# A diffusion step on one core: modulation steps moved between TensorE and VectorE

## The chip, the core and the metric

The kernel runs on one core of a Trainium2 chip. A core has five engines that run side by side, each with its own queue of instructions: TensorE (PE in the profile, with its weight loads as PEld) multiplies matrices into PSUM, VectorE (DVE) and ScalarE (ACT) do elementwise work, GpSimd (POOL) some more of it, and SyncE (SP) starts transfers; all of them can start transfers between HBM and the on-chip memory SBUF. The metric is the time of one execution in microseconds (us) on the device: the median of three runs of the kernel before is 1942.72 us, from 1942.26 to 1943.35.

## The reference

One layer of a hybrid diffusion model, in float32, for 128 context tokens and 256 latent tokens, width 2048:

```python
mod = silu(cond) @ w_ada + b_ada                 # six vectors of 2048 per condition
sh1, sc1, ga1, sh2, sc2, ga2 = split(mod, 6)
h = rmsnorm(x) * (1 + sc1) + sh1
q, k, v, g, lr_f, lr_b, fo = split(h @ w_in)
o = bidirectional gated linear attention (GLA) of q, k, v with decays from lr_f, lr_b   # 4 heads
o = rmsnorm per head(o) * gla_out_norm * silu(g)
f = real part of the 2-D DFT of fo, per group
gates = sigmoid(h @ w_gate + b_gate)
m = (g_a * (o @ w_br_gla) + g_b * (f @ w_br_four)) @ w_out
x = x + ga1 * rmsnorm(m)
h = rmsnorm(x) * (1 + sc2) + sh2
x = x + ga2 * rmsnorm((silu(h @ w_ffn_gate) * (h @ w_ffn_up)) @ w_ffn_down)
```

There are two conditions, one for the context and one for the latent tokens, so `mod` is a product of a 2 x 2048 matrix with a 2048 x 12288 one: little arithmetic on many weights. The output also holds the final GLA states.

## The kernel before

Activations lie with channels on the 128 partitions and all 384 tokens along the row (`T = 384`). The large products are done in three passes on reduced-precision halves: ScalarE casts a weight tile `raw` of 128x1024 to `whi` (line 300), VectorE makes the rest `wlo = raw - whi` (line 287), and TensorE multiplies `whi` with both halves of the activation and `wlo` with the high one (line 326, tile `pmm`). `whi` and `wlo` have four buffers each, so a weight tile can be made up to four units ahead of its use. A *half unit* is one such weight tile with its 24 matmuls; a *unit* of an output column block has two of them where the contraction is 2048 long, and one where it is 1024 long (the branch units).

The order of each engine's instructions is that in which the code emits them, since the kernel schedules PE, ACT, DVE and POOL by hand. The stages are: the first two modulation vectors with the v, q and k projections; the GLA, interleaved with q, k and merge-gate projections; the rest of the merge gates with the Fourier input; the *output gates* (`("o", i)` in `mix_order`, eight units of two half units, `turn` 0 to 15); the *branch units* (`("a", i)`, sixteen units of one half unit, with the last Fourier units `("b", i)` between them); the output projection; the feed-forward part.

The modulation vectors 2, 3 and 4 are made along the way by the generator `ada_rest` (lines 685 to 723). It works on six pieces of 1024 columns, each of 16 *steps*. A step loads 512 KB of `w_ada` into one of two buffers `adaw` (a transfer on POOL's queue) and then does one of two things:

- on PE, if `on_pe[0]` is true: four matmuls into the PSUM tile `pr` (line 697), which stays open until the piece is done;
- else on DVE: two `scalar_tensor_tensor` rows that add the weighted tile to `adacc` (line 707), or for the first step of a piece two `tensor_scalar` rows (line 705).

After 16 steps comes one turn of the generator without work, then one that adds `adacc` into `pr` on PE (line 718) and copies it on ACT (`adev`, line 667), then the next turn begins with two transposes (`ptm`, line 671) and small DVE rows that write `mods` (lines 676 to 681), and goes on with the first step of the next piece.

The generator is advanced by the loops around it. In the GLA, `side` advances `gla()` and then the modulation by one at the end of each half unit. In the output gates another `side` does so at `turn` 0 to 8 and at 9, 11, 13 and 15. In the branch units the table `TAIL` names the units that begin with a step, with True for PE and False for DVE. The output projection runs through what is left.

In the output gates, each odd half unit is followed by `gcol`: transposes of the GLA output (`pt`, line 1196), a Silu on ACT (line 1198), and on DVE `gs` (line 1199) and `o_lo`. A Fourier unit `four(i)` (lines 1239 to 1252) follows from the third output gate on behind each half unit. Its weight tile is folded by VectorE first (`ws`, lines 243 and 244), and then cast and split like the others. In the branch units VectorE multiplies the gate with the product (line 1296), adds (line 1297) and makes `A_lo`, the low half of the output projection's input.

Of the kernel before, what the change touches and what calls it, by code (L numbers as in the profile page):

```python
# [37 lines left out]
XU = 2  # L38
GF = 25
GD = 256  # L40
TAIL = {1: True, 4: False, 5: True, 8: True, 10: False, 11: True, 13: True, 14: False, 15: False}


C_TRI = 0
# [63 lines left out]
def tile_step(ctx: ExitStack, tc: tile.TileContext, a, o):  # L108
# [209 lines left out]
    def step(side):  # L318
        if side is not None:
            next(side, None)  # L320
# [27 lines left out]
    def proj(pool, x, dst, side=None, mid=()):  # L348

        p = pool.tile([P, T], F32, tag="mm", name="pmm")  # L350
        for g in range(2):
            gemm(p, grab(), x, 8, k0=8 * g, first=g == 0, last=g == 1)
            while later:
                later.pop()()
            if g:
                later.append(lambda: dst(p))
            step(side)
            if not g:
                for unit in mid:
                    unit()  # L360
# [5 lines left out]
    def paced(gen, rate):  # L366

        due = 0.0
        while True:
            due += rate[0]  # L370
            while due >= 1.0:
                due -= 1.0
                if next(gen, 1) is not None:
                    return
            yield
# [307 lines left out]
    on_pe = [False]  # L683
# [68 lines left out]
    ada = paced(ada_gen, rate)  # L752
    with ExitStack() as s:
# [22 lines left out]
        def chunks(x):  # L776
            return x.rearrange("p (t c i) -> p t c i", t=3, c=2)

        def gla():
# [10 lines left out]
            for h in range(NH):  # L790
# [38 lines left out]
                for d in range(2):  # L829


                    bT = pss.tile([P, T], F32, tag="side", name="bT")
                    for t in range(3):
                        for j, l in enumerate((lah, lal)):
                            PE.matmul(
                                bT[:, t * P : (t + 1) * P], l[:, t, d], tri[:, d * P : (d + 1) * P],
                                start=j == 0, stop=j == 1,
                            )
                    sx = pss.tile([P, 2, P], F32, tag="side", name="sx")
                    for j, l in enumerate((lah, lal)):  # L840
                        PE.matmul(
                            sx, tri[:, (2 + d) * P : (3 + d) * P], l[:, 0 : 2 + d : 1 + d, d], start=j == 0, stop=j == 1,
                        )
                    eb = pg.tile([P, T], F32, tag=f"eb{d}", name="eb")
                    ACT.activation(eb, bT, AF.Exp)
                    ki = pg.tile([P, T], F32, tag=f"ki{d}", name="ki")
                    ACT.activation(ki, bT, AF.Exp, scale=-1.0)
                    ko = pg.tile([P, 2, P], F32, tag=f"ko{d}", name="ko")
                    ACT.activation(ko, sx, AF.Exp)
                    qi = pg.tile([P, T], F32, tag=f"qi{d}", name="qi")  # L850
                    DVE.scalar_tensor_tensor(qi, eb, DK**-0.5, qT[:, h, :], op0=ALU.mult, op1=ALU.mult)
                    DVE.tensor_mul(ki, ki, kT[:, h, :])
                    DVE.tensor_mul(ko, ko, krs[:, 0 : 2 + d : 1 + d, :])

                    last = 0 if d else CH - 1
                    tot = chunks(eb)[:, :, d, last : last + 1]
                    kc = pg.tile([P, 3, CH], F32, tag=f"kc{d}", name="kc")
                    DVE.tensor_mul(kc, chunks(ki)[:, :, d, :], tot.to_broadcast([P, 3, CH]))
                    dc = pg.tile([P, 1], F32, tag=f"dc{d}", name="dc")
                    c = 5 if d else 2  # L860
                    e0, e1 = c * CH + last, (c + 1 - 2 * d) * CH + last
                    DVE.tensor_mul(dc, eb[:, e0 : e0 + 1], eb[:, e1 : e1 + 1])
                    qin.append(qi)
                    kin.append(ki)
                    kcr.append(kc)
                    kout.append(ko)
                    dec.append((tot, dc))
                    yield

                ats = []  # L870
                for d in range(2):
# [89 lines left out]
        for c in range(2):  # L961
# [4 lines left out]
            DVE.tensor_scalar_mul(dst, up.bitcast(F32), coef[0:98, 1:2])  # L966
            DVE.scalar_tensor_tensor(dst, raw, coef[0:98, 0:1], dst.bitcast(F32), op0=ALU.mult, op1=ALU.add)
        gl = gla()
        def side():
            while True:  # L970
                next(gl, None)
                next(ada, None)
                yield

        sd = side()
# [117 lines left out]
    with ExitStack() as s:  # L1093
# [83 lines left out]
        turn = [0]  # L1177

        def side():
            while True:  # L1180
                on_pe[0] = turn[0] > 6 and turn[0] != 8
                if turn[0] < 9 or turn[0] % 2:
                    next(ada_gen, None)
                on_pe[0] = False
                turn[0] += 1
                next(df, None)
                next(nw, None)
                yield
# [71 lines left out]
        for b, i in mix_order:  # L1260
# [18 lines left out]
            else:  # L1279
# [3 lines left out]
                if i == KT - 3:  # L1283
                    depth[0] = 2
                    spare_raws.clear()
                if i in TAIL:
                    on_pe[0] = TAIL[i]
                    next(ada_gen, None)
# [21 lines left out]
    with ExitStack() as s:  # L1310
# [518 lines left out]
        ada = paced(ada_last(), rate)  # L1829
        pd_tiles, hid_last, x1b, done = None, None, None, 0  # L1830
        for kind, c, i in steps[:-4]:
# [8 lines left out]
            if kind == "D":  # L1840
# [9 lines left out]
                h = hid_last if last_c else hid  # L1850
# [248 lines left out]
```

## Time and profile before

| | |
|---|---|
| median of three runs | 1942.72 us (1942.26 to 1943.35) |
| the profiled execution | 1942.28 us |
| its span, first to last instruction | 1940.4 us |
| granted TensorE clock, mean | 0.998 of full speed |
| steps on PE in the output gates and branch units | 5 and 5 |
| steps on DVE in the output gates and branch units | 6 and 4 |

A page of the profile gives busy times of the engines; its other views list groups of equal instructions, waits and what ended them, the chain of work that ended last, and rows in order of time. A row of the timeline has its start in us, its length, the engine, the line of the code, the operation, the tiles written and read, their shape, how many equal ones were merged, and in brackets the idle time of that engine just before, with what ended it. The end of a row can lie up to 0.1 us behind the start of the next on VectorE and ScalarE, and more on TensorE, since these work on in a pipeline. A busy TensorE is not TensorE at its peak.

### The profile page before, as it was taken

What the parts mean: (1) busy time and instruction counts of PE and PEld (TensorE: products, weight loads), DVE (VectorE), ACT (ScalarE), POOL (GpSimd) and SP (SyncE); (2) the same over time, 40 slices, a digit from 0 to 9 for tenths busy, and PEclk for the clock granted to TensorE, in tenths of its full rate; (3) what the DMA queues carried; (4) which work ended last, traced back from release to release, by engine and by line L of the source; (5) the groups of instructions that cost most, each with busy time, mean ns of one, the idle gap of its engine ahead of it and who ended that gap; (6) DMA issues with size and microseconds to landing.
All of it is one profiled execution on the core that took longest, in us unless ns stands there. A gap on an engine that the chain in (4) does not pass through costs nothing.

```text
span 1940.4 us, 27538 instructions
## 1 busy us (share of the span) xinstructions
PE 1920.4 (99%) x10534; PEld 1690.8 (87%) x10534; DVE 1647.8 (85%) x2172; ACT 916.3 (47%) x1298; POOL 85.8 (4%) x154
## 2 busy tenths in 40 slices
PE   9999999999999999999999999999999999999997
PEld 5779999999999999999988888888888888888886
DVE  5668898889878887978789888999998999888885
ACT  4235455545456554456455444444444444444444
POOL 0001111100000000104000000000000000000001
PEclk9999999999999999999999999999999999999999
DMA  9977766766757885755264636363636272625243
GB/s 390 387 260 248 240 234 227 248 231 194 225 185 246 302 302 181 245 193 198 83 195 131 200 103 194 121 211 98 216 104 213 91 222 93 201 76 185 87 173 110
DMA packets 200615, 380.52 MB, mean 196 GB/s; under 512 B 14196, under 2 KB 126932, under 8 KB 196132
## 3 DMA queue, kind: packets, MB, share of 16 engines
q1 hardware_dynamic: 181252, 320.84, 48.9%
q0 software_dynamic: 13952, 50.39, 8.5%
q10 hardware_dynamic: 5280, 7.55, 1.1%
q8 instruction: 82, 1.34, 0.3%
q14 instruction: 49, 0.40, 0.1%
HBM read 361.94 MB, written 16.78 MB: 195 GB/s over the span
## 4 chain that ended last, share of the span: by engine, by line
PE 93%; DVE 3%; DMA 2%; issue 1%; ACT 1%; SPq 0%; DVEq 0%; ACTq 0%
PE pgu L338 30%; PE pmm L326 30%; PE pdn L338 18%; PE pv L491 3%; PE pgm L474 1%; PE pf L1239 1%; PE pfo L1039 1%; DVE adacc L707 1%; PE pmm L1516 1%; PE ptr L1808 1%; PE pf L1240 1%; PE pfo L1040 1%; DMA xraw<-in_w_x 1%; PE po L788 1%; PE px L509 0%
## 5 line engine op out<-in xcount | busy, mean ns | idle before, releaser
L326 PE MATMUL pmm<-A_hi,whi 128*128 128x384 f32 x1072 | 361.7, 337 | 0.0
L326 PE MATMUL pmm<-A_hi,wlo 128*128 128x384 f32 x1072 | 358.8, 335 | 0.0
L326 PE MATMUL pmm<-A_lo,whi 128*128 128x384 f32 x1072 | 358.6, 335 | 0.0
L1663 ACT CAST whi<-u 128x1024 fp32r<-128x1024 f32 x200 | 210.6, 1053 | 281.5 <-DVE u L1647 86.5
L1663 ACT CAST whi<-raw 128x1024 fp32r<-128x1024 f32 x175 | 184.2, 1052 | 200.8 <-PE pgu L338 63.8
L1674 DVE TENSOR_TENSOR wlo<-u,whi 128x1024 fp32r<-128x1024 f32 x200 | 244.1, 1220 | 32.0 <-ACT whi L1663 18.3
L338 PE MATMUL pgu<-whi,A_hi 128*128 128x512 f32 x640 | 250.0, 391 | 0.0
L338 PE MATMUL pgu<-whi,A_lo 128*128 128x512 f32 x640 | 249.3, 389 | 0.0
L1674 DVE TENSOR_TENSOR wlo<-raw,whi 128x1024 fp32r<-128x1024 f32 x175 | 213.4, 1220 | 34.6 <-ACT whi L1663 25.6
L287 DVE TENSOR_TENSOR wlo<-raw,whi 128x1024 fp32r<-128x1024 f32 x163 | 198.2, 1220 | 24.1 <-ACT whi L300 23.7
L300 ACT CAST whi<-raw 128x1024 fp32r<-128x1024 f32 x149 | 156.0, 1051 | 117.6 <-PE pmm L326 50.0
L326 PEld LDWEIGHTS pmm<-A_hi,whi 128*128 128x128 f32 x1072 | 201.2, 188 | 3.3 <-issue 2.5
L326 PEld LDWEIGHTS pmm<-A_lo,whi 128*128 128x128 f32 x1072 | 201.4, 188 | 0.2
L326 PEld LDWEIGHTS pmm<-A_hi,wlo 128*128 128x128 f32 x1072 | 201.2, 188 | 0.3 <-DVE wlo L287 0.2
L707 DVE SCALAR_TENSOR_TENSOR adacc<-adaw,spad,adacc 128x1024 f32<-128x1024 f32 x160 | 198.1, 1279 | 3.5 <-DMA adaw<-in_w_ada 3.2
L338 PE MATMUL pdn<-whi,hid_hi 128*128 128x512 f32 x480 | 186.9, 389 | 0.0
L338 PE MATMUL pdn<-whi,hid_lo 128*128 128x512 f32 x480 | 186.8, 389 | 0.0
L338 PE MATMUL pgu<-wlo,A_hi 128*128 128x512 f32 x640 | 184.2, 389 | 0.0
L338 PEld LDWEIGHTS pgu<-whi,A_hi 128*128 128x128 f32 x640 | 120.2, 188 | 26.1 <-issue 0.8
L338 PEld LDWEIGHTS pgu<-wlo,A_hi 128*128 128x128 f32 x640 | 120.1, 188 | 25.4
L338 PEld LDWEIGHTS pgu<-whi,A_lo 128*128 128x128 f32 x640 | 120.1, 188 | 25.0
L338 PE MATMUL pgu<-whi,S 128*128 128x512 f32 x480 | 131.1, 395 | 0.0
(405 smaller groups left out, 3042.7 us busy)
## 6 DMA issues: line engine op xcount, KB each, us to landing
adaw<-in_w_ada POOLq DMA_DIRECT2D x96, 512.0 KB, 4.0
raw<-in_w_d SPq DMA_DIRECT2D x88, 512.0 KB, 3.7
slab<-in_w_ada SPq DMA_DIRECT2D x32, 1024.0 KB, 10.2
raw<-in_w_gate SPq DMA_DIRECT2D x64, 512.0 KB, 4.4
raw<-in_w_g SPq DMA_DIRECT2D x48, 512.0 KB, 3.4
raw<-in_w_u SPq DMA_DIRECT2D x48, 512.0 KB, 3.5
raw<-in_w_in SPq DMA_DIRECT2D x44, 512.0 KB, 4.3
u<-in_w_u SPq DMA_DIRECT2D x40, 512.0 KB, 4.6
```

The source lines that it names most:

```text
L287: eng.tensor_sub(lo, raw, hi.bitcast(F32))
L300: ACT.copy(hi, raw)
L326: PE.matmul(dst, w[wi][:, k * n + n0 : k * n + n0 + P], x[xi][:, k0 + k, :], start=first and k == 0 and j == 0, stop=last and k == kts - 1 ...
L338: PE.matmul(dst, stat[x_][m], mov(w[w_], m), start=first and w_ == m == x_ == 0, stop=last and w_ == m == 1,)
L474: PE.matmul(pgv[q : q + 32, :], spad[:, k, :], slab[k // (KT // 2)][:, k % (KT // 2), :], start=k < 4, stop=k >= KT - 4,)
L491: PE.matmul(pv[2 * t + g], hT[x_][:, kb, t * P : (t + 1) * P], w_[:, g * 512 : (g + 1) * 512], start=kb == 0 and j == 0, stop=kb == KT - 1 ...
L707: DVE.scalar_tensor_tensor(acc[:, c, :], w, spad[:, k, c : c + 1], acc[:, c, :], op0=ALU.mult, op1=ALU.add,)
L788: PE.matmul(dst, w[wi], x[xi], start=first and j == 0, stop=last and j == 2)
L1039: PE.matmul(p, w_of[0][:, i, k, g, :], x[:, :, lo:hi], start=kt == 0, stop=False)
L1040: PE.matmul(p[:, 0], w_of[1][:, i, k, g, :], x[:, 0, lo:hi], start=False, stop=kt == KT - 1)
L1663: ACT.copy(hi, src)
L1674: DVE.tensor_sub(lo, src, hi.bitcast(F32))
```

## The change

```diff
-TAIL = {1: True, 4: False, 5: True, 8: True, 10: False, 11: True, 13: True, 14: False, 15: False}
+TAIL = {1: False, 4: False, 5: False, 7: False, 8: False, 10: False, 11: False, 13: False, 14: False, 15: False}
@@ in gla(), the loop over the two directions d of a head h
                     dec.append((tot, dc))
-                    yield
+                    yield h == 0 and d == 0
@@ in side() of the GLA stage
-                next(gl, None)
-                next(ada, None)
+                if not next(gl, None):
+                    next(ada, None)
@@ in side() of the output gates
-                on_pe[0] = turn[0] > 6 and turn[0] != 8
+                on_pe[0] = turn[0] > 12
```

In the GLA stage one half unit of the first head, the one that prepares direction 0, no longer takes a step. All later turns of the generator come one place later, until the new entry 7 in `TAIL` brings it level again; behind unit 7 of the branch units the same step is done at the same place as before. The choice of engine changes as well:

| place | steps before | steps now |
|---|---|---|
| first GLA head, direction 0 | 1 on DVE | none |
| output gates, `turn` 0 to 4 | 5 on DVE | 5 on DVE |
| `turn` 5 | a turn without work | 1 on DVE |
| `turn` 6 | `adacc` into `pr`, copy `adev` | a turn without work |
| `turn` 7 | `mods`, first step of a piece, on PE | `adacc` into `pr`, copy `adev` |
| `turn` 8 | 1 on DVE (line 705) | `mods`, first step of a piece, on DVE (line 705) |
| `turn` 9 and 11 | 2 on PE | 2 on DVE |
| `turn` 13 and 15 | 2 on PE | 2 on PE |
| branch units 1, 5, 8, 11, 13 | 5 on PE | 5 on DVE |
| branch unit 7 | none | 1 on DVE |
| branch units 4, 10, 14, 15 | 4 on DVE | 4 on DVE |

So eight steps go from PE to DVE. Where the rows stand on VectorE is shown at three places. The first is the first GLA head, between the rows of direction 0 (`kc`, `dc`) and those of direction 1 (`qi`):

```order
 L858 TENSOR_TENSOR kc<-ki,eb 128x192
 L862 TENSOR_TENSOR dc<-eb 128x1
-L707 SCALAR_TENSOR_TENSOR adacc<-adaw,spad,adacc 128x1024 x2
 L287 TENSOR_TENSOR wlo<-raw_1706,whi 128x1024
 L851 SCALAR_TENSOR_TENSOR qi<-eb,qk 128x384
```

The step ahead of the weight split and of direction 1 is gone. The second place is VectorE in the output gates around `turn` 9, from the fold of a Fourier weight (`ws`) to the weight splits, before and then now:

```order
L243 TENSOR_TENSOR ws<-raw 128x512
L244 TENSOR_TENSOR ws<-raw 128x512
L1199 SCALAR_TENSOR_TENSOR gs<-gs,gnorm,pt 128x384
L379 TENSOR_TENSOR o_lo<-gs,o_hi 128x384
L287 TENSOR_TENSOR wlo<-ws,whi 128x1024
L287 TENSOR_TENSOR wlo<-raw,whi 128x1024
```

```order
L243 TENSOR_TENSOR ws<-raw 128x512
L244 TENSOR_TENSOR ws<-raw 128x512
L707 SCALAR_TENSOR_TENSOR adacc<-adaw,spad,adacc 128x1024 x2
L1199 SCALAR_TENSOR_TENSOR gs<-gs,gnorm,pt 128x384
L379 TENSOR_TENSOR o_lo<-gs,o_hi 128x384
L287 TENSOR_TENSOR wlo<-ws,whi 128x1024
L287 TENSOR_TENSOR wlo<-raw,whi 128x1024
```

The step stands between the fold and `gs`; it does so at `turn` 5, 9 and 11. The third place is VectorE in the branch units, from the last row of Fourier unit 13 to the weight splits behind branch unit 8, before and then now:

```order
L1252 TENSOR_TENSOR y<-y,gate 128x384
L243 TENSOR_TENSOR ws<-raw 128x512
L244 TENSOR_TENSOR ws<-raw 128x512
L1296 TENSOR_TENSOR gate<-gate,pmm 128x384
L1297 TENSOR_TENSOR yb<-yb,gate 128x384
L379 TENSOR_TENSOR A_lo<-yb,A_hi 128x384
L287 TENSOR_TENSOR wlo<-ws,whi 128x1024
L287 TENSOR_TENSOR wlo<-raw,whi 128x1024
```

```order
L1252 TENSOR_TENSOR y<-y,gate 128x384
L707 SCALAR_TENSOR_TENSOR adacc<-adaw,spad,adacc 128x1024 x2
L243 TENSOR_TENSOR ws<-raw 128x512
L244 TENSOR_TENSOR ws<-raw 128x512
L1296 TENSOR_TENSOR gate<-gate,pmm 128x384
L1297 TENSOR_TENSOR yb<-yb,gate 128x384
L379 TENSOR_TENSOR A_lo<-yb,A_hi 128x384
L707 SCALAR_TENSOR_TENSOR adacc<-adaw,spad,adacc 128x1024 x2
L287 TENSOR_TENSOR wlo<-ws,whi 128x1024
L287 TENSOR_TENSOR wlo<-raw,whi 128x1024
```

The step of unit 7 is new, and that of unit 8 comes from TensorE: between these two Fourier units VectorE now has two steps where it had none.

## The prediction

> **What bounds the kernel.** The page first: shares of busy time, and the chain that ended last.
>
> ```profile
> PE 1920.4 (99%) x10534; PEld 1690.8 (87%) x10534; DVE 1647.8 (85%) x2172; ACT 916.3 (47%) x1298; POOL 85.8 (4%) x154
> PE 93%; DVE 3%; DMA 2%; issue 1%; ACT 1%; SPq 0%; DVEq 0%; ACTq 0%
> ```
>
> TensorE (PE) is the bound nearly everywhere, so work taken off it counts in full, as long as VectorE (DVE) keeps up. The change does take work off PE, and gives it to DVE. So the second view is busy time by stage: the first GLA head, the output gates from half unit 4 on, the branch units, the start of the output projection.
>
> ```profile
> core 0: us, PE busy (x) PEld busy (x) DVE busy (x) ACT busy (x) POOL busy (x), PEclk, DMA share, GB/s
> 145.00:195.00 50.00, 48.45 (x313) 47.69 (x312) 42.99 (x51) 26.14 (x36) 5.02 (x10) 1.00 0.73 249
> 571.00:655.00 84.00, 84.00 (x553) 79.75 (x554) 71.62 (x143) 53.98 (x85) 3.69 (x7) 1.00 0.74 243
> 655.00:738.00 83.00, 83.00 (x514) 79.87 (x513) 73.15 (x123) 41.01 (x68) 4.74 (x9) 1.00 0.88 309
> ```
>
> In both stages that receive steps PE never pauses, but DVE has only 12.4 us (84.00 - 71.62) and 9.9 us (83.00 - 73.15) free. Whether a step fits there is the whole question.
>
> **Prices of one step.** On PE, from the timeline in the branch units:
>
> ```profile
> 708.32 0.33 PE L326 MATMUL pmm<-o_lo,whi 128*128 128x384 f32 x1
> 708.49 0.34 PE L326 MATMUL pmm<-o_hi,wlo 128*128 128x384 f32 x1
> 708.76 0.64 PE L697 MATMUL pr<-adaw,spad 128*32 128x256 f32 x8
> 709.33 0.45 PE L326 MATMUL pmm<-o_hi,whi 128*128 128x384 f32 x1
> ```
>
> From the last matmul before it to the first after it are 0.84 us, against a pitch of 0.17: a step costs PE 0.67 us. On DVE, a step and the row behind it, and then the load that it needs (issue to landing):
>
> ```profile
> 706.88 2.47 DVE L707 SCALAR_TENSOR_TENSOR adacc<-adaw,spad,adacc 128x1024 f32<-128x1024 f32 x2
> 709.27 0.69 DVE L243 TENSOR_TENSOR ws<-raw 128x512 f32<-128x512 f32 x1
> adaw<-in_w_ada POOLq DMA_DIRECT2D x96, 512.0 KB, 4.0
> ```
>
> A step costs DVE 709.27 - 706.88 = 2.39 us. Eight steps move: 8 x 0.67 = 5.4 us come off PE, 8 x 2.39 = 19.1 us go onto DVE, and as one GLA step goes, the two late stages receive nine (three in the output gates, six in the branch units), 21.5 us against 22.3 us of idle time. That looks as if it just fitted; the next parts ask which of that idle time can be used.
>
> **First GLA head: a gain.** VectorE's and TensorE's rows there, then the same products of a later head:
>
> ```profile
> 188.77 2.47 DVE L707 SCALAR_TENSOR_TENSOR adacc<-adaw,spad,adacc 128x1024 f32<-128x1024 f32 x2
> 191.16 1.21 DVE L287 TENSOR_TENSOR wlo<-raw,whi 128x1024 fp32r<-128x1024 f32 x1
> 192.77 0.54 DVE L852 TENSOR_TENSOR ki<-ki,qk 128x384 f32<-128x384 f32 x1
> 191.34 0.57 PE L875 MATMUL at<-qi,ki 128*64 128x64 f32 x12
> 193.46 0.57 PE L875 MATMUL at<-qi,ki 128*64 128x64 f32 x12 [1.55 <-DVE ki L852]
> 193.83 0.71 PE L881 MATMUL cr<-qi,kc 128*64 128x64 f32 x12
> 328.56 0.92 PE L875 MATMUL at<-qi,ki 128*64 128x64 f32 x24
> 329.31 0.52 PE L881 MATMUL cr<-qi,kc 128*64 128x64 f32 x12
> ```
>
> PE waits 1.55 us for `ki`, behind the very step that goes. Without it `ki` ends at 193.31 - 2.39 = 190.92, before the products begin at 191.34. They take 193.83 - 191.34 = 2.49 us here and 0.75 in the later head: **-1.7 us**. The load of that step goes too. All later steps of the GLA move by one half unit; there PE never waits, so I count that as nothing.
>
> **Output gates.** One round is two half units, an even and an odd one, each followed by the Fourier products of one unit; behind the odd one DVE has the row `gs` (L1199), which needs that unit's Silu from ScalarE (ACT). The `gs` at 606.78 is that of half unit 9, the one at 621.01 that of half unit 11. DVE over this round, then ACT's rows at its begin, then the first PE matmul that needs the `wlo` made there:
>
> ```profile
> 606.01 0.69 DVE L244 TENSOR_TENSOR ws<-raw 128x512 f32<-128x512 f32 x1
> 606.78 0.61 DVE L1199 SCALAR_TENSOR_TENSOR gs<-gs,gnorm,pt 128x384 f32<-128x384 f32 x1
> 607.98 0.56 DVE L379 TENSOR_TENSOR o_lo<-gs,o_hi 128x384 fp32r<-128x384 f32 x1 [0.58 <-ACT o_hi L378]
> 608.93 1.23 DVE L287 TENSOR_TENSOR wlo<-ws,whi 128x1024 fp32r<-128x1024 f32 x1 [0.39 <-ACT whi L294]
> 615.59 1.23 DVE L287 TENSOR_TENSOR wlo<-ws,whi 128x1024 fp32r<-128x1024 f32 x1 [1.17 <-ACT whi L294]
> 621.01 0.61 DVE L1199 SCALAR_TENSOR_TENSOR gs<-gs,gnorm,pt 128x384 f32<-128x384 f32 x1
> 606.25 0.49 ACT L1198 ACTIVATE gs<-pmm 128x384 f32<-128x384 f32 x1
> 607.43 0.52 ACT L378 CAST o_hi<-gs 128x384 fp32r<-128x384 f32 x1 [0.68 <-DVE gs L1199]
> 607.85 1.05 ACT L294 CAST whi<-ws 128x1024 fp32r<-128x1024 f32 x1
> 612.53 0.25 PE L1240 MATMUL pf<-edT,wlo 128*128 128x194 f32 x1
> ```
>
> DVE's only pauses in a round (0.58, 0.39, 1.17) are waits for ACT casts that themselves wait for the DVE row just before. DVE and ACT thus form one chain of 621.01 - 606.78 = 14.23 us, as long as PE's round, and a step in front of `gs` lengthens it: the pauses don't shrink. The new steps of half units 9 and 11 stand exactly there: VectorE takes its rows in order, so `gs`, the two casts, both `wlo` and the rows of `y` behind them all move back by the step. Only 0.16 us is free at the first (L244 lets the next row start at about 606.62, `gs` waits until 606.78) and nothing at the second. The cushion is the lead of `wlo`: it ends at 608.93 + 1.23 = 610.16 and is needed at 612.53, so 2.37 us.
>
> Half unit 5 gets a step as well, before a `gs` whose ACT input is ready early; and at half unit 7 the small rows of `mods` leave the place before `gs`:
>
> ```profile
> 577.64 0.61 DVE L1199 SCALAR_TENSOR_TENSOR gs<-gs,gnorm,pt 128x384 f32<-128x384 f32 x1
> 575.76 0.49 ACT L1198 ACTIVATE gs<-pmm 128x384 f32<-128x384 f32 x1 [2.31 <-PE pmm L326]
> 591.80 0.23 DVE L676 COPY mods<-ptm 128x8 f32<-128x8 f32 x2
> 592.33 0.61 DVE L1199 SCALAR_TENSOR_TENSOR gs<-gs,gnorm,pt 128x384 f32<-128x384 f32 x1
> ```
>
> DVE's lateness against the profile: +2.39 (half unit 5); -0.53 where `mods` left (592.33 - 591.80) and +0.45 where it lands in half unit 8; +2.39 - 0.16 (half unit 9); +2.39 (half unit 11): 6.9 us. PE waits for all but the lead: 6.9 - 2.4 = **4.5 us late** when the branch units begin. The 0.67 us that PE saves at half units 7, 9 and 11 only let it come earlier to that wait, so I count them as zero (if that cover is gone, they are worth 2.0 us); so too the `pr` bank that stays free until half unit 13. ACT copies `adev` at half unit 7 instead of 6, ahead of its Silu, which delays the Silu by some 1.1 us; `gs` is later than that anyway.
>
> **Branch units.** DVE's row that waits for PE, all 16 units together, and DVE's last row against the matmul that needs it:
>
> ```profile
> L1296 DVE TENSOR_TENSOR gate<-gate,pmm 128x384 f32<-128x384 f32 x16 | 8.8, 551 | 8.5 <-PE pmm L326 8.5
> 736.47 1.23 DVE L379 TENSOR_TENSOR A_lo<-yb,A_hi 128x384 fp32r<-128x384 f32 x2
> 741.39 0.33 PE L326 MATMUL pmm<-A_lo,whi 128*128 128x384 f32 x1
> ```
>
> Here the idle time is real: 8.5 us of waiting for PE, which vanish once DVE is the later one. Six more steps are 14.3 us, so the lateness grows by 14.3 - 8.5 = 5.8 to 12.7 us. The output projection needs the last `A_lo` at 741.39, and it ends at 737.70: a lead of 3.7. PE is therefore 12.7 - 3.7 = **9.0 us late**, for good, since PE is again the bound from there on. The branch matmuls saved (5 x 0.67) vanish in the wait again. Their loads go out two steps ahead; the shortest notice, two steps before unit 15, is some 7 us against 4.0 to land. SP's weight loads wait for `wlo` to free a buffer and move with DVE, never by more.
>
> **Sum.** +9.0 - 1.7 = +7.3 on the profiled execution, 1942.28 (span 1940.4), which is 0.4 under the median: 1949.6, or about 1949.9 by the median. I say 1949.8. Bounds: the GLA term 0 to -1.9 (the idle 1.55 and what the `cr` row shows over its later twin); the stages from +2.1 (only the branch units cost) to +12.7 (no lead helps).
>
> **Rivals.** *Faster:* DVE swallows the steps, PE keeps 5.4 + 1.7: 1935.6. For it speaks that the sums nearly fit (21.5 in 22.3); against it that 2.1 us of each 14.2 are waits inside DVE's own chain. It decides by whether a lead of 2.37 outlasts a step of 2.39 in front of `gs`. *No change:* the output gates hide their three steps, the branch units alone cost 5.8 - 3.7 = 2.1: 2.1 - 1.7, 1943.1. *Slower still:* the clock falls. New PE pauses near half units 9 and 11 last 1 to 2 us each, at two neighbouring matmuls; if the clock halved after both, the 2.4 us of Fourier products behind each would double: +4.8, 1954.6. Against it: the granted clock is 1.00 in the window that holds the 1.55 us pause. The Trainium skill (TensorE: Matmul & The Clock Gate, Why this matters for your kernels) warns of idle gaps over about 3 us, after which the clock is halved; no run here shows a gap of that length. By that rule my pauses are too short, and the sum stays as it is.
>
> **How the numbers follow.** Likeliest 70%; slower still 9%; no change 11%; faster 10%. A difference under 0.2% (3.9 us) can't be told from none. The range drops the faster case and some of the slowest: 1943 to 1955; the likeliest alone gives 1946.5 to 1953. Slower: 70 + 9 + a little of the no-change case = 0.81; same 0.10; faster 0.09.
>
> **What would show it.** Right: no pause before `at` in the first head; PE pauses at the Fourier products (L1239, L1240) that end with DVE `wlo` or ACT `whi`, 4.5 us in all by the start of the branch units; L1296 no longer waits for PE; DVE almost without idle time from 571 to 750; the output projection starts some 7 us later. Wrong: L1240 still has a positive lead after half unit 9, or L1296 still waits.

## The result, and the profile after

The changed kernel takes 1949.39 us in the median of five runs (1948.73 to 1950.28), against 1942.72. It is slower by 6.7 us; forecast were 7.1. The ratio over all runs is 1.0036, with a 95% interval of 1.0026 to 1.0047 (ratios here and below are over all runs, and differ from those of the medians by up to 0.0003). Its profiled execution took 1950.06 us with a span of 1948.3, so 0.67 more than the median and 7.9 more span than the one before.

First the page of the changed kernel, then busy time in the three stages of the prediction (the third is drawn out to where the changed kernel ends the branch units).

```profile
PE 1920.5 (99%) x10470; PEld 1693.6 (87%) x10470; DVE 1665.3 (85%) x2188; ACT 915.4 (47%) x1298; POOL 85.8 (4%) x154
PE 88%; DVE 6%; DMA 3%; ACT 2%; issue 1%; SPq 0%; DVEq 0%; ACTq 0%
```

```profile
145.00:195.00 50.00, 50.00 (x324) 49.34 (x323) 43.42 (x53) 25.80 (x36) 5.02 (x10) 1.00 0.71 245
571.00:655.00 84.00, 78.57 (x485) 74.79 (x484) 72.55 (x138) 47.61 (x74) 3.43 (x7) 0.96 0.66 215
655.00:745.00 90.00, 86.70 (x508) 86.06 (x507) 88.10 (x140) 44.00 (x75) 5.01 (x10) 0.98 0.91 309
```

PE's busy time over the whole span is the same to 0.1 us although eight steps are gone, since it now also runs at a lower granted clock for a while (0.96 and 0.98 in these windows, 1.00 before); and 5.4 us (84.00 - 78.57) and 3.3 us of idle time have come into two stages that had none. DVE's share of the chain that ended last has doubled to 6%. The view of waits on PE says who is late:

```profile
PE pf L1240 <- DVE wlo L287: 5.6, 5, 1.9
PE pf L1239 <- ACT whi L294: 3.2, 2, 1.7
PE pmm L326 <- DVE wlo L287: 0.4, 1, 0.4
```

(us in total, times, longest.) In the first head the pause before `at` is gone: DVE and PE there, with `ki` written by 190.46 and all 24 matmuls of `at` in one go:

```profile
189.91 0.55 DVE L852 TENSOR_TENSOR ki<-ki,qk 128x384 f32<-128x384 f32 x1
191.05 2.48 DVE L707 SCALAR_TENSOR_TENSOR adacc<-adaw,spad,adacc 128x1024 f32<-128x1024 f32 x2
191.34 0.92 PE L875 MATMUL at<-qi,ki 128*64 128x64 f32 x24
```

In the output gates the rows `gs` are the milestones: those of half units 5, 7, 9, 11, 13 and 15, with three rows of the kernel before behind them.

```profile
578.76 0.61 DVE L1199 SCALAR_TENSOR_TENSOR gs<-gs,gnorm,pt 128x384 f32<-128x384 f32 x1
592.92 0.61 DVE L1199 SCALAR_TENSOR_TENSOR gs<-gs,gnorm,pt 128x384 f32<-128x384 f32 x1
607.56 2.48 DVE L707 SCALAR_TENSOR_TENSOR adacc<-adaw,spad,adacc 128x1024 f32<-128x1024 f32 x2
609.96 0.61 DVE L1199 SCALAR_TENSOR_TENSOR gs<-gs,gnorm,pt 128x384 f32<-128x384 f32 x1
611.14 0.56 DVE L379 TENSOR_TENSOR o_lo<-gs,o_hi 128x384 fp32r<-128x384 f32 x1 [0.58 <-ACT o_hi L378]
612.09 1.23 DVE L287 TENSOR_TENSOR wlo<-ws,whi 128x1024 fp32r<-128x1024 f32 x1 [0.39 <-ACT whi L294]
618.76 1.23 DVE L287 TENSOR_TENSOR wlo<-ws,whi 128x1024 fp32r<-128x1024 f32 x1 [1.17 <-ACT whi L294]
626.56 0.61 DVE L1199 SCALAR_TENSOR_TENSOR gs<-gs,gnorm,pt 128x384 f32<-128x384 f32 x1
641.51 0.62 DVE L1199 SCALAR_TENSOR_TENSOR gs<-gs,gnorm,pt 128x384 f32<-128x384 f32 x1 [0.67 <-ACT gs L1198]
655.74 0.61 DVE L1199 SCALAR_TENSOR_TENSOR gs<-gs,gnorm,pt 128x384 f32<-128x384 f32 x1
```

```profile
554.53 0.61 DVE L1199 SCALAR_TENSOR_TENSOR gs<-gs,gnorm,pt 128x384 f32<-128x384 f32 x1 [2.18 <-PE pt L1196]
635.23 0.62 DVE L1199 SCALAR_TENSOR_TENSOR gs<-gs,gnorm,pt 128x384 f32<-128x384 f32 x1
649.46 0.61 DVE L1199 SCALAR_TENSOR_TENSOR gs<-gs,gnorm,pt 128x384 f32<-128x384 f32 x1
```

The three pauses of a round (0.58, 0.39, 1.17) have not shrunk by a hundredth though a step of 2.48 stands before them. Before the gates begin, `gs` stands 1.27 us earlier than before (553.26 against 554.53). From there it falls back by 2.39 at half unit 5 (578.76 - 577.64 = +1.12), gains 0.53 (592.92 against 592.33), loses 2.59 (609.96 against 606.78), 2.37 (626.56 against 621.01), and 0.73 more (641.51 against 635.23), where no step stands but where `gs` waited 0.67 us for its Silu. In sum 7.55.

PE's pauses there, besides one of 0.64 us at 582.18 behind the step of half unit 5, and the granted clock from one of them on:

```profile
612.11 0.45 PE L1239 MATMUL pf<-edT,whi 128*128 128x388 f32 x1 [1.43 <-ACT whi L294]
613.37 0.36 PE L1240 MATMUL pf<-edT,wlo 128*128 128x194 f32 x1 [0.81 <-DVE wlo L287]
628.71 0.45 PE L1239 MATMUL pf<-edT,whi 128*128 128x388 f32 x1 [1.73 <-ACT whi L294]
629.97 0.53 PE L1240 MATMUL pf<-edT,wlo 128*128 128x194 f32 x1 [0.81 <-DVE wlo L287]
```

```profile
629.97:636.24 6.27, 6.27 (x22) 6.27 (x23) 5.04 (x11) 3.85 (x6) 0.00 (x0) 0.50 0.57 172
...
725.05:728.50 3.45, 3.45 (x15) 3.45 (x15) 3.42 (x5) 1.47 (x3) 0.00 (x0) 0.52 1.01 308
```

Behind the pauses of 1.73 and 0.81 us PE ran 6.27 us at half its clock (22 matmuls, some 3 us more than at full clock), and behind one of 1.85 us in the branch units again for 3.4 us. And the branch units: L1296 over the whole program, and the end of the stage.

```profile
L1296 DVE TENSOR_TENSOR gate<-gate,pmm 128x384 f32<-128x384 f32 x16 | 8.8, 548 | 0.0
733.10 2.48 DVE L707 SCALAR_TENSOR_TENSOR adacc<-adaw,spad,adacc 128x1024 f32<-128x1024 f32 x2
735.50 1.22 DVE L287 TENSOR_TENSOR wlo<-raw,whi 128x1024 fp32r<-128x1024 f32 x1
747.80 1.22 DVE L379 TENSOR_TENSOR A_lo<-yb,A_hi 128x384 fp32r<-128x384 f32 x2
749.25 0.33 PE L326 MATMUL pmm<-A_lo,whi 128*128 128x384 f32 x1
```

L1296 never waits any more. The last `A_lo` is written at 749.02, 11.3 us later than the 737.70 of before, and PE comes to the matmul that needs it at 749.25, 7.86 us later than the 741.39 of before; from there to the end the shift stays as it is (7.9 in the span).

### The profile page after: what moved, and what is told of

It is laid out like the page before. It is cut to its first block, busy times and chain, and to the rows that moved or that the text cites. A ratio compares the mean times of both kernels' runs of the same rounds, so it can differ in the third digit from the quotient of the medians.

```text
span 1948.3 us, 27434 instructions
## 1 busy us (share of the span) xinstructions
PE 1920.5 (99%) x10470; PEld 1693.6 (87%) x10470; DVE 1665.3 (85%) x2188; ACT 915.4 (47%) x1298; POOL 85.8 (4%) x154
## 3 DMA queue, kind: packets, MB, share of 16 engines
q10 hardware_dynamic: 5280, 7.55, 1.1%
## 4 chain that ended last, share of the span: by engine, by line
PE 88%; DVE 6%; DMA 3%; ACT 2%; issue 1%; SPq 0%; DVEq 0%; ACTq 0%
PE pgu L338 30%; PE pmm L326 27%; PE pdn L338 18%; PE pv L491 3%; PE pgm L474 1%; DVE adacc L707 1%; DVE wlo L287 1%; PE pfo L1039 1%; PE pmm L1516 1%; DMA four_d<-y 1%; PE ptr L1808 1%; DMA xraw<-in_w_x 1%; PE po L788 1%; PE pf L1239 0%; PE px L509 0%
## 5 line engine op out<-in xcount | busy, mean ns | idle before, releaser
L326 PE MATMUL pmm<-A_hi,whi 128*128 128x384 f32 x1072 | 362.1, 338 | 0.0
L326 PE MATMUL pmm<-A_hi,wlo 128*128 128x384 f32 x1072 | 359.3, 335 | 0.4 <-DVE wlo L287 0.4
L326 PE MATMUL pmm<-A_lo,whi 128*128 128x384 f32 x1072 | 359.0, 335 | 0.0
L338 PE MATMUL pgu<-whi,A_hi 128*128 128x512 f32 x640 | 250.0, 391 | 0.0
L338 PE MATMUL pgu<-whi,A_lo 128*128 128x512 f32 x640 | 249.3, 389 | 0.0
L707 DVE SCALAR_TENSOR_TENSOR adacc<-adaw,spad,adacc 128x1024 f32<-128x1024 f32 x176 | 217.9, 1280 | 2.8 <-DMA adaw<-in_w_ada 2.5
L326 PEld LDWEIGHTS pmm<-A_hi,whi 128*128 128x128 f32 x1072 | 201.6, 188 | 3.3 <-issue 2.5
L326 PEld LDWEIGHTS pmm<-A_hi,wlo 128*128 128x128 f32 x1072 | 201.5, 188 | 1.0 <-DVE wlo L287 0.9
L326 PEld LDWEIGHTS pmm<-A_lo,whi 128*128 128x128 f32 x1072 | 201.7, 188 | 0.2
L338 PE MATMUL pdn<-whi,hid_hi 128*128 128x512 f32 x480 | 186.9, 389 | 0.0
L338 PE MATMUL pdn<-whi,hid_lo 128*128 128x512 f32 x480 | 186.8, 389 | 0.0
L338 PE MATMUL pgu<-wlo,A_hi 128*128 128x512 f32 x640 | 184.2, 389 | 0.0
L338 PEld LDWEIGHTS pgu<-whi,A_hi 128*128 128x128 f32 x640 | 120.1, 188 | 26.0 <-issue 0.8
L338 PEld LDWEIGHTS pgu<-wlo,A_hi 128*128 128x128 f32 x640 | 120.1, 188 | 25.4
L338 PEld LDWEIGHTS pgu<-whi,A_lo 128*128 128x128 f32 x640 | 120.1, 188 | 25.1
L338 PE MATMUL pgu<-whi,S 128*128 128x512 f32 x480 | 131.1, 395 | 0.0
```

Of the source, the lines that this page charges most:

```text
L326: PE.matmul(dst, w[wi][:, k * n + n0 : k * n + n0 + P], x[xi][:, k0 + k, :], start=first and k == 0 and j == 0, stop=last and k == kts - 1 ...
L338: PE.matmul(dst, stat[x_][m], mov(w[w_], m), start=first and w_ == m == x_ == 0, stop=last and w_ == m == 1,)
L707: DVE.scalar_tensor_tensor(acc[:, c, :], w, spad[:, k, c : c + 1], acc[:, c, :], op0=ALU.mult, op1=ALU.add,)
```

## The experiments

My theory, as in the prediction: VectorE's rows form a chain; a step lengthens it by its 2.39 us unless it stands where VectorE really waits for another engine, and PE pays what the lead doesn't cover. The rivals: VectorE's load alone decides (the steps fit into its idle time or not, wherever they stand); and the halved clock is what costs the time. All medians below are of kernels timed beside the kernel before on the same chip, which took 1942.57 us there (1942.59 in the last group).

**The GLA part alone.** The step that is left over goes to branch unit 7.

```diff
-TAIL = {1: True, 4: False, 5: True, 8: True, 10: False, 11: True, 13: True, 14: False, 15: False}
+TAIL = {1: True, 4: False, 5: True, 7: False, 8: True, 10: False, 11: True, 13: True, 14: False, 15: False}
-                    yield
+                    yield h == 0 and d == 0
-                next(gl, None)
-                next(ada, None)
+                if not next(gl, None):
+                    next(ada, None)
```

> The GLA part alone (the step that it leaves over is added in branch unit 7, on VectorE). My theory: PE no longer waits 1.55 us for `ki` (a gain of 1.7), the changed kernel's new 0.4 us pause before the Fourier-input products comes with it, and the added step of 2.39 us fills idle time of L1296 (4.2 us of it lie in units 6 to 9). In all 1.3 us less: about 1941.4. Rival: the wait only moves to another product, no change, 1942.7. Rival: the added step is not covered, 2.39 - 1.3 = 1.1 more, 1943.8.

Measured: 1941.53 us (1940.58 to 1942.37, 11 runs), ratio 0.9993, interval 0.9984 to 1.0002. It is 1.0 us less, near the 1.3 of my theory, though the interval takes in no change; the trace shows what happened: no wait for `ki`, and one at L326, here of 0.9.

```profile
PE pmm L326 <- DVE wlo L287: 0.9, 1, 0.9
```

That wait, at some 520 us, comes and goes with the execution: it is there with 0.63 us in the next kernel, too, whose GLA is that of before.

**The output gates alone.**

```diff
-                on_pe[0] = turn[0] > 6 and turn[0] != 8
+                on_pe[0] = turn[0] > 12
```

> The output gates alone (branch units and GLA as before). By the step of the prediction, PE is 4.5 us late at the begin of the branch units and nothing there gives it back: 1947.2. If the halved clock that the changed kernel shows after its pause at 626.64 is a real loss, PE is 7.5 us late there (the shift of 6.28 at 635 plus the 1.27 of the GLA), 1950.2. Rival (load: VectorE has 12.4 us free in this stage and swallows three steps of 2.39): PE keeps 3 x 0.67, 1940.7.

Measured: 1948.94 us (1948.76 to 1950.5, 5 runs), ratio 1.0032 (1.0019 to 1.0044): 6.4 more. That VectorE swallows the steps is refuted. The value lies between my two numbers, and the trace shows the same pair of pauses with the clock behind them: first the two matmuls, then the windows on both sides.

```profile
614.13 0.45 PE L1239 MATMUL pf<-edT,whi 128*128 128x388 f32 x1 [1.98 <-ACT whi L294]
615.39 0.36 PE L1240 MATMUL pf<-edT,wlo 128*128 128x194 f32 x1 [0.81 <-DVE wlo L287]
```

```profile
611.00:615.40 4.40, 1.60 (x9) 1.02 (x7) 3.43 (x5) 2.78 (x5) 0.53 (x1) 1.00 0.83 240
615.40:619.60 4.20, 4.20 (x19) 4.20 (x20) 4.13 (x10) 1.87 (x3) 0.00 (x0) 0.61 0.58 181
```

VectorE's `gs` falls back by 6.8 us here (+1.16 at half unit 7, +3.29 at 9, +2.37 at 11): other terms than the prediction's, and nearly its sum. PE begins the branch units 4.6 us late (656.19 against 650.83, in an execution that stood 0.75 us later at the begin of the gates), which is 6.8 less a lead of 2.2, and it is 4.7 late at the matmul with the last `A_lo`. So the theory's 4.5 holds, and the halved clock has cost next to nothing by then: PE was going to wait for VectorE anyway. The rest of the 6.4 comes later: in the profiled execution, the slowest of the five, another 2.8 us come in behind the output projection, of them 1.1 in a wait for `psums` (L338) that only some of the profiles here show.

**Everything but the output gates.**

```diff
-                on_pe[0] = turn[0] > 12
+                on_pe[0] = turn[0] > 6 and turn[0] != 8
```

(against the changed kernel)

> The change without its output-gate part. My theory: six steps of 2.39 less 8.5 idle make VectorE 5.8 us late at the last `A_lo`, less the lead of 3.7 is 2.1, less 1.3 from the GLA: 0.8 more, 1943.5; L1296 no longer waits, and the granted clock stays 1.00 in the output gates. Rival (load): all of it fits, 5 x 0.67 + 1.3 = 4.7 less, 1938.0. Rival: the branch units alone cost the 9.0 us that the prediction gave both stages together, 1950.4.

Measured: 1945.05 us (1944.0 to 1945.81, 11 runs), ratio 1.0010 (1.0001 to 1.0019): 2.5 more, where I had said 0.8. My sum had left out that the GLA part brings a step to half unit 5 of the output gates, in this kernel too. `gs` therefore enters the branch units 2.0 us late (2.39 - 0.53 + 0.19; within the lead, so PE doesn't wait at that place; it does wait 0.64 us at half unit 5), and the sum is 2.0 + 5.0 - 3.7 = 3.3 for PE. The trace has that: PE's matmul with the last `A_lo` but one starts 2.9 us later than before (743.81 against 740.87) in an execution that stood 0.3 us earlier at the begin of the gates, and here it does wait for it.

```profile
743.81 0.44 PE L326 MATMUL pmm<-A_lo,whi 128*128 128x384 f32 x1 [1.09 <-DVE A_lo L379]
```

The 5.0 replaces the prediction's 5.8 (14.3 - 8.5). The idle times shown for L1296 run from the end of the row before, and rows that stand back to back overlap by up to 0.1 us (733.10 + 2.48 = 735.58, while the next begins at 735.50). Each of the nine waits is worth that much more to a later VectorE: 8.5 + 9 x 0.09 = 9.3. In this kernel the clock stayed at 1.00 behind two pauses of 1.85 us, and the loss is still there: here the clock is not what makes it.

```profile
700.00:703.00 3.00, 1.37 (x8) 1.04 (x7) 3.00 (x3) 1.97 (x4) 0.53 (x1) 1.00 0.77 213
703.00:706.50 3.50, 3.28 (x22) 3.28 (x23) 3.47 (x6) 1.11 (x3) 0.00 (x0) 1.00 1.02 336
```

**The branch units alone.** Nine steps as before, all on VectorE.

```diff
-TAIL = {1: True, 4: False, 5: True, 8: True, 10: False, 11: True, 13: True, 14: False, 15: False}
+TAIL = {1: False, 4: False, 5: False, 8: False, 10: False, 11: False, 13: False, 14: False, 15: False}
```

> The branch units alone: the nine steps of before, all on VectorE (five more there), GLA and output gates as before. My theory: 5 x 2.39 = 12.0, less the 9.3 of idle time that the kernel without the output-gate part showed to be usable, makes the last `A_lo` 2.65 us late; PE comes to it 5 x 0.67 = 3.35 earlier; the lead of 3.7 covers 0.35 of the 2.65, so PE waits 2.3 and keeps 1.05: 1941.6. Rival: what the kernel without the output-gate part lost there comes from the six steps themselves (3.3 for six, so some 2.8 for five): 1945.4.

Measured: 1941.47 us (1940.67 to 1942.21, 11 runs), ratio 0.9993 (0.9984 to 1.0002). The forecast was 1941.6, the rival's 1945.4. Five steps more on VectorE in the same stage cost no time; six of them behind a VectorE that enters 2.0 us late cost some 3 us. The difference is the lead: PE waits 1.1 us for the last `A_lo` but one and 1.2 for one `wlo`, and saves five steps of 0.67.

```profile
PE pf L1240 <- DVE wlo L287: 1.2, 1, 1.2
PE pmm L326 <- DVE A_lo L379: 1.1, 1, 1.1
```

**The same steps one half unit later.** The changed kernel, with the VectorE steps of the output gates where a round has its longest pause.

```diff
-                if turn[0] < 9 or turn[0] % 2:
+                if turn[0] < 9 or turn[0] in (10, 12, 13, 15):
```

> The changed kernel, but the VectorE steps of half units 9 and 11 of the output gates stand one half unit later (10 and 12), between a fold `ws` and its `wlo`, where VectorE waits 1.17 us for the cast in each round. My theory (a chain of VectorE and ScalarE rows, not VectorE's load): each of these two steps then lengthens the chain by 2.39 - 1.17 = 1.22 instead of 2.39. VectorE starts the branch units 2.39 - 0.53 + 0.45 + 2 x 1.22 = 4.75 us late (7.55 in the changed kernel), 5.04 more there, less the lead of 3.7: PE 6.1 late, less 1.3 of the GLA: 4.8 more than before, 1947.4, some 3 us under the changed kernel's profiled execution; pauses of PE in the output gates of some 2.4 us in all. Rival (load): the same number of the same rows in the same stage, so the changed kernel's time, 1949.4.

Measured: 1947.24 us (1946.19 to 1947.94, 9 runs), ratio 1.0024 (1.0015 to 1.0034); 1947.4 was forecast by the chain, 1949.4 by load. The row below stands where the wait of 1.17 us was:

```profile
614.03 0.68 DVE L244 TENSOR_TENSOR ws<-raw 128x512 f32<-128x512 f32 x1
614.64 2.47 DVE L707 SCALAR_TENSOR_TENSOR adacc<-adaw,spad,adacc 128x1024 f32<-128x1024 f32 x2
617.03 1.22 DVE L287 TENSOR_TENSOR wlo<-ws,whi 128x1024 fp32r<-128x1024 f32 x1
622.43 0.61 DVE L1199 SCALAR_TENSOR_TENSOR gs<-gs,gnorm,pt 128x384 f32<-128x384 f32 x1
637.77 0.61 DVE L1199 SCALAR_TENSOR_TENSOR gs<-gs,gnorm,pt 128x384 f32<-128x384 f32 x1
```

`wlo` no longer waits, and from one `gs` to the next are 637.77 - 622.43 = 15.34 us instead of 14.23: the step costs the chain 1.11 us, not 2.39. The same work in the same stage, moved by half a round, is worth 2 us; the load is not the price. Nor is it the clock that makes the 1.11: it stays at 1.00 in this profile, and in that of the changed kernel the two steps had cost their 2.59 and 2.37 before it fell.

**Four steps more on VectorE in the branch units,** with the GLA part.

```diff
-TAIL = {1: True, 4: False, 5: True, 8: True, 10: False, 11: True, 13: True, 14: False, 15: False}
+TAIL = {1: False, 4: False, 5: True, 7: False, 8: False, 10: False, 11: True, 13: False, 14: False, 15: False}
```

> GLA as changed, output gates as before, and in the branch units four steps more on VectorE (1, 7, 8, 13), not six; 5 and 11 stay on TensorE. My theory: the idle time of L1296 before and behind these units takes all but 1.5 us of their 9.6, the lead of 3.7 (less the 2.0 that PE saves) covers that, so PE keeps 3 x 0.67 = 2.0 and the 1.3 of the GLA: 3.3 less, 1939.4. Rival: VectorE's idle time is not usable, 9.6 - 3.7 - 1.3 = 4.6 more, 1947.3.

Measured: 1941.13 us (1940.55 to 1942.91, 11 runs), ratio 0.9991 (0.9983 to 1.0000): 1.4 less, not 3.3. The rival that the idle time isn't usable falls; my number was too good: it again left out the 2.0 us of half unit 5, and took 1.3 for the GLA. VectorE enters the branch units 2.0 us late and is 2.2 late at the last `A_lo`, so the four steps cost it 0.25 us there, which is 4 x 2.39 less the 9.3 found above.

**That step of half unit 5 back on PE.** Against the kernel just told:

```diff
-                on_pe[0] = turn[0] > 6 and turn[0] != 8
+                on_pe[0] = turn[0] > 4 and turn[0] not in (6, 8)
```

> The kernel with four steps more on VectorE in the branch units (GLA as changed), and half unit 5's step of the output gates, which the GLA part brought there, on TensorE. My theory: the step costs PE 0.67 and takes away both the pause that it made (0.78 more between two matmuls at 582) and 2.31 us of VectorE's lateness, so that PE no longer waits for the last `A_lo` (0.4 there): 0.5 less than the kernel with four steps more, and no PE pause from 560 on. About 1940.6. Rival: that step was hidden where it was, so this one is 0.67 longer: 1941.8.

Measured: 1940.95 us (1939.47 to 1944.81, 11 runs), ratio 0.9991 (0.9982 to 1.0000). In the trace no PE pause is left between 560 and 745, as forecast, and PE starts the output projection some 3 us earlier than before. Of these, 0.5 remain in the span of that execution: PE waits 0.91 us at 984 and 0.76 at 1886, waits that some of the other profiles here show and some do not. It is the best of all kernels here by its median, 1.6 us under the kernel before; between it and the one with the step on VectorE no difference can be told.

**Which pauses lose the clock.** The kernel before, with pauses put into PE (core of the edit; the last line for the second kernel):

```diff
+        def pause(n):
+            for k in range(2):
+                px_ = pss.tile([P, 64], F32, tag="side", name="pz")
+                PE.matmul(px_, ident, z[:, 0:64], start=True, stop=True)
+                if not k:
+                    for _ in range(n):
+                        POOL.memset(z, 0.0)
...
+                if n > 12 and n % 3 == 0:
+                    pause((2, 4, 5, 6, 8, 10)[n // 3 % 6])
...
+                    pause(5)
```

> The kernel before with 15 pauses put into PE, some 19 us apart, behind half units of the first projections: a matmul on a small tile, 2 to 10 fills of that tile by GpSimd, and a matmul that needs the last fill (they add work and change no result). It asks which pauses are followed by a halved granted clock. If length alone decides, all pauses above some length between 1.6 and 1.9 us (the changed kernel kept the clock after 1.55 and lost it after 1.85) lose it and none below. If it is a matter of where the pause falls in time, pauses of the same length come out both ways. By the rule of the Trainium skill (TensorE: Matmul & The Clock Gate, Why this matters for your kernels: gaps over about 3 us) only the longest would lose it. Time: the sum of the pauses, some 30 us, and up to 3 us behind each that loses the clock.

> The kernel with 15 added pauses again, now all of one length (five fills; such a pause had PE idle for 1.96 us, and kept the clock once and lost it once). If length decides, all 15 come out the same way. If it is a matter of where in time a pause falls, some lose the clock and some keep it. Time: some 30 us for the pauses, and some 2 us behind each that loses the clock.

(The 1.55 us of the first text is the pause of the kernel before; the changed kernel kept the clock after 1.44.) The two took 2005.66 and 1994.41 us (one execution each), 63 and 52 more than the kernel before; the pauses (33.4 and 29.6 us) and the halved clock explain all but some 10 of that in each. Counted by the granted clock in the 4.5 us behind each pause, over both kernels:

| PE idle, us | pauses | followed by a halved clock |
|---|---|---|
| 0.86 | 3 | 0 |
| 1.59 | 3 | 2 |
| 1.90 to 1.96 | 16 | 7 |
| 2.25 to 2.33 | 3 | 3 |
| 3.07 | 2 | 2 |
| 3.74 to 3.81 | 3 | 3 |

Two pauses of equal length in the second kernel, the matmul that ends each and the window behind it:

```profile
247.79 0.43 PE L976 MATMUL pz<-z,ident 128*128 128x64 f32 x2 [1.96 <-POOL z L979]
300.81 0.43 PE L976 MATMUL pz<-z,ident 128*128 128x64 f32 x2 [1.96 <-POOL z L979]
```

```profile
247.80:252.30 4.50, 4.50 (x19) 4.50 (x20) 0.26 (x1) 3.69 (x5) 1.04 (x2) 0.65 0.63 220
300.82:305.32 4.50, 4.50 (x28) 4.50 (x29) 4.03 (x5) 1.41 (x4) 1.05 (x2) 1.00 0.75 193
```

So length alone doesn't decide between 1.6 and 2 us; from 2.25 us on every pause here lost the clock. What does decide can be read from the times at which the clock changes. Within a run, whatever the pause, all of them lie a multiple of 3.41 us apart, and every fall ahead of the program's end lasts 3.41 or 6.83 us: the clock is set anew at fixed moments, whose place differs from run to run. The same two pauses, cut at these moments:

```profile
245.78:249.19 3.41, 1.45 (x11) 1.40 (x11) 0.00 (x0) 1.42 (x3) 2.60 (x7) 1.00 0.34 124
249.19:252.60 3.41, 3.41 (x12) 3.41 (x12) 0.56 (x1) 3.20 (x4) 0.00 (x0) 0.50 0.87 305
296.98:300.39 3.41, 1.86 (x12) 1.73 (x10) 2.94 (x7) 0.59 (x2) 1.25 (x4) 1.00 0.41 137
300.39:303.81 3.42, 3.00 (x20) 3.00 (x21) 3.42 (x4) 1.14 (x2) 1.30 (x3) 1.00 0.63 168
```

The first pause lies within one such window (3.41 - 1.45 = 1.96 us idle), and the next window is halved; the second is split into 1.55 and 0.42, and nothing follows. Over the eleven traces, without the windows that begin in the first 3 us, full-clock windows with up to 1.58 us of idle PE never had a halved one behind them, those with 1.85 and more always had (28 of 28), and of the 13 between, 3 had. Pauses in one window add up: the changed kernel's 1.73 and part of its 0.81 make 2.16. And its pause of 1.85 lay within one window, while those of 1.85 in the kernel without the output-gate part and in the shifted one were split (0.91 and 0.94, or 0.55 and 1.30). Why 3 of the 20 falls last two windows stays open.

## Why the prediction was right

Forecast was 1949.8, within 1943.0 to 1955.0, slower at 0.81; it took 1949.39. Point by point:

- *GLA, -1.7:* the pause went as said; the term was too large. At the begin of the output gates the profiled execution stands 1.27 us earlier than before, since 0.4 come back in a pause at L326. Alone it is worth 1.0 us in the medians. The pause in the profile of before was also a long one: in the two kernels here that leave the GLA as it was, PE waits only 0.8 us for `ki`. Two small slips of the sum: by the median it gives 1942.72 + 7.3 = 1950.0, not 1949.9, and the bound of -1.9 comes out of its rows as 1.55 + 0.19 = 1.74.
- *Output gates, 6.9 for VectorE:* the terms 2.39, -0.53, +0.45 + 2.39 - 0.16 and 2.39 came out as 2.39, -0.53, 2.59 and 2.37. Missing was a fifth of 0.73: with PE at half clock, the product of half unit 13 and its Silu came late to `gs`. In all 7.55.
- *PE 4.5 late at the begin of the branch units:* this is the step that failed. PE was 7.55 late (657.11 against 650.83 at the first matmul, and 1.27 for the earlier begin), just as late as VectorE's `gs` (655.74 against 649.46): of the lead of 2.4 nothing was left. The pauses were there, at L1239 and L1240 and ended by `whi` and `wlo`, but the clock fell behind the second pair, which I had as the rival "slower still" and thought unlikely, as a pause of 1.55 us had kept it; the fall lasted 6.83 us, two windows, and behind it PE made no further pause in that stage, since it was itself the late one. With the output gates alone it lasted one window, PE paused once more behind it, and was 4.6 late. The prediction's sentence on the rule of the Trainium skill (TensorE: Matmul & The Clock Gate, Why this matters for your kernels), that such pauses are too short, is not borne out either.
- *Yet the total stands,* because it goes by VectorE's chain. It ended 11.32 + 1.27 = 12.6 us late, forecast 12.7: the gates gave 0.65 more, the branch units 5.04 for 5.8. Less the lead of 3.7 are 8.9 for PE; measured are 7.86 + 1.27 = 9.1. That the gates' surplus and the branch units' shortfall offset each other is luck. By this sum the 3 us that the clock took from PE early are for the most part time that it would else have waited for VectorE in the branch units; what the fall did cost is the 0.73 in VectorE's chain. No run takes the fall of the clock away by itself, so that stays an argument, but the record bears it out. The profiled execution, with a mean clock of 0.995, had three halved windows ahead of the program's end and took 1950.06 us. The two executions with a mean of 0.998 have room for one at most (0.998 is at most 9.7 us at half clock in all, and the end of the program alone has 5.3 to 8.0 of it in the profiles here), and they took 1950.28 and 1948.82 us. And with the output gates alone PE was no later at the branch units than VectorE's 6.8 us and the lead give, though its clock was halved for 3.4 us.
- *Where PE pays:* the prediction let it wait at the last `A_lo`. It waited before, at the Fourier products in the branch units (1.44 and 1.85 us), and came to `A_lo` 0.2 us after it was written. Where the clock kept full speed, as without the output gates, PE paused on the way too (1.17, 1.85 and 1.85 us) and still waits 1.09 us for the last `A_lo` but one.
- *The PE steps counted as zero:* right for the changed kernel. The gain is there only as long as VectorE keeps its lead, as in the kernels with four and five steps more.
- *The rivals:* "faster" by load falls with the shifted steps and the output gates alone; "no change" had the output gates hide their steps, which they did not; "slower still" had the event right and its price of 4.8 us wrong.

## What to carry to other kernels

Before work is moved to an engine with idle time, look at what that idle time is. A wait for a cast that waits for the row just before is part of a chain and takes nothing in; a wait for the engine that bounds the kernel does, and so does the lead of the last result, once. And a step belongs behind the row whose answer the engine is going to wait for, not in front of it: here half a round made 2.39 us into 1.11.

## What was not expected of the hardware

- The granted clock fell to half after PE pauses of 1.6 to 2 us, in 9 of 19 such pauses put in on purpose, and after all eight of 2.25 us and more; the same length came out both ways. Each fall lasted 3.41 us or twice that, on a grid of 3.41 us that keeps its place through a run and has another in the next; what counts is how long PE is idle within one such window (up to 1.58 us kept the clock, 1.85 and more lost it). The Trainium skill (TensorE: Matmul & The Clock Gate, Part 1: The HAM clock gate) tells of an activity window that runs free of the program; that pauses of one length come out both ways, by their place on the grid, agrees with it, that 1.6 us can do does not agree with the 3 us of its advice.
- By the sum of VectorE's chain, the two falls of the clock in the changed kernel (some 4.8 us of slower matmuls) lengthened it by the 0.73 us of one late Silu only: PE was going to wait for VectorE further on, and the slow matmuls took that waiting time.
